# Transposes issued by SyncE instead of ScalarE, value planes prepared one weight tile sooner, and a shorter last normalisation, in a one-core streaming encoder layer

## The chip, the core and the metric

The kernel runs on one core of a Trainium2 chip. The core has five engines, each with its own instruction queue that runs in order: TensorE (PE in the profile, its weight loads as PEld), VectorE (DVE), ScalarE (ACT), GpSimd (POOL) and SyncE (SP), which only issues transfers. Sixteen DMA engines move data between HBM and the on-chip memory SBUF, for all queues together. SyncE, ScalarE and GpSimd can issue DMAs. The metric is device time in microseconds for one execution.

## The reference

One layer of a streaming encoder is applied to two request groups that share the weights: 256 new frames of a prompt and 64 next frames of a running stream with 256 cached rows of keys and values. Inputs and weights are float32, and the model width is 2048.

```python
def layer(x, l, cache_k, cache_v, ...):
    xn = rmsnorm(x, norm_mix[l])
    proj = xn @ w_in[l]
    q, k, v, u, vs, g = jnp.split(proj, ...)      # 8 heads x 128 each for q, k, v; 1024 for u, vs; 4096 for g
    a = stick_breaking(...)                       # prompt: own keys; sample: cache + own keys
    u = jax.nn.gelu(u)
    vs = rmsnorm(jax.nn.gelu(vs), sgu_norm[l])
    bb = spatial_gate(u, vs, w_spatial[l], b_spatial[l])
    gates = jax.nn.sigmoid(g + b_gate[l])
    merged = g_a * (a @ w_branch_a[l]) + g_b * (bb @ w_branch_b[l])
    h = x + merged @ w_out[l]
    gu = rmsnorm(h, norm_ffn[l]) @ w_gate_up[l]
    h = h + (silu(gu[..., :D_FF]) * gu[..., D_FF:]) @ w_down[l]     # D_FF = 5632
    return h, k, v, vs

def stick_breaking_block(q_blk, q_pos, k, v, k_pos):
    z = einsum(q_blk, k) * (SB_HEAD_DIM ** -0.5)
    mask = k_pos[None, :] < q_pos[:, None]
    log_beta = log_sigmoid(z)
    log_stay = where(mask, log_sigmoid(-z), 0.0)
    log_rest = cumsum(log_stay, reverse=True) - log_stay
    w = where(mask, exp(log_beta + log_rest), 0.0)
    return einsum(w, v)
```

The outputs are the final RMSNorm of `h` for both groups, the new k and v rows of both, and the normalised `vs` rows of the sample.

## The kernel before

**Layout.** Features lie on the 128 partitions, and the T = 320 frames (256 prompt, 64 sample) lie along the free dimension. A weight matrix is cut into blocks of 128 output columns; for every such block the kernel walks the contraction in *weight tiles* of eight 128x128 blocks (512 KB). `weights` (line 74) loads a tile on SyncE into a buffer `raw`, and `halved` (line 66) splits it in two: `wh`, a rounded copy that ACT writes (line 69, a "cast"), and `wl`, the rest, which VectorE computes (line 70, a "split"). Activations are split the same way. `product` (line 83) then issues three matmuls for each 128x128 block: high by high, high by low, low by high (lines 86 to 88), so that float32 accuracy is kept on a faster number format. A tile therefore feeds 24 matmuls of 320 columns.

**Buffers.** There are three `raw` buffers, and three more (`raw2`) while the attention pool is open, and four each of `wh` and `wl`. A new weight tile is issued when the split of an older tile has freed its buffer. A cast waits until TensorE has done with an older `wh`.

**Ticks.** `block` (line 90) computes one block of 128 output columns, and after each weight tile it calls `tick()`. Other work is hung on later ticks with `at(tick, function, ...)`: it is then traced between two weight tiles. Which instruction of an engine goes first is decided when the program is built, by when each is expected to be ready; `keep_in_program_order` pins an instruction behind what was traced before it on its engine. At run time each queue is fixed and runs in order.

**Attention.** Heads are treated in pairs p = 0 to 3. After a pair's k, q and v blocks, `attend` (line 380) hangs up its steps: `att_scores` (TensorE, masks, and the activations on ACT), `att_sums` (the reversed running sums, on VectorE), `att_values`, `att_weights`, `att_plane`, `att_join` and `att_out`. The attention weights `w` and the values `v` must be transposed. Both are float32, and the DMA transpose moves 16-bit elements, so each is taken as two 16-bit *planes*:

- `turn_begin` (line 260), called by `att_values` for the values, and by `sgu_turn` for the rows of the spatial gate: four ACT copies collect the planes of two heads in `flat` (lines 264 and 267), then one DMA transpose writes `turned` (line 269, issued by ACT). `turn_end` puts the planes together again on VectorE (line 277).
- `att_weights` applies the exponential on ACT (line 318) and calls `att_plane(p, 0)`; two ticks later comes `att_plane(p, 1)`. Each copies one plane of `w` into `e` on ACT (line 326) and transposes it into `c` (line 327, issued by ACT).
- `att_join` (line 329) puts the planes of `c` together on VectorE (line 334) and calls `turn_end` for the values. `att_out` (line 340) is the product with the values.

There are 16 transposes: two of `c` and one of `turned` for each of four pairs, and four of `turned` for the spatial gate, about 70 to 317 us after the start.

**The end.** The last `w_down` slice adds to `hs[m]` block by block (line 536). The squares of blocks 0 to 14 are summed in `sqf.total`, those of the last block stand in `last` (line 544), and each `hs[m]` is multiplied by its gain (line 545). Then six matmuls against a column of ones sum both square tiles over the partitions, into one PSUM bank (line 551). ACT takes the square root of the mean (line 553), VectorE writes the mean itself (line 554), and `newton` (line 130: a reciprocal and three small steps, lines 131 to 134) makes an accurate reciprocal root `r`, one value per frame, with frames on partitions. To bring `r` back along the free dimension, VectorE scales an identity by it (`diag`, line 559) and TensorE multiplies a matrix of ones by that (line 560). Sixteen VectorE multiplies of 128x320 (line 562) and nine DMAs issued by SyncE (line 566) follow. A float32 matmul appears as two passes in the profile.

Of the kernel before, what the change touches and what calls it, by code (L numbers as in the profile page):

```python
# [8 lines left out]
F32 = mybir.dt.float32  # L9
F32R = mybir.dt.float32r  # L10
U16 = mybir.dt.uint16
AF = mybir.ActivationFunctionType
ALU = mybir.AluOpType

P = 128
TP = 256
TS = 64
T = TP + TS
D = 2048
KD = D // P  # L20
# [6 lines left out]
EPS = 1e-6  # L27
# [6 lines left out]
def stream_step(ctx: ExitStack, tc: tile.TileContext, xT, w_in, w_a, w_b, w_out, w_gu, w_down,  # L34
                gains, ws_t, bs, ck_t, cv, y_t, k_t, v_t, sv_t):
    nc = tc.nc
# [5 lines left out]
    tmp = pool("tmp", 2)  # L42
# [5 lines left out]
    def aux():  # L48
        return psum.tile([P, 512], F32, tag="aux", bufs=4, name="aux")

    def aux1():
        return psum.tile([P, 512], F32, tag="aux1", bufs=1, name="aux1")
# [4 lines left out]
    def at(tick, fn, *a):  # L57
        assert tick > state["tick"], (tick, state["tick"])
        later.setdefault(tick, []).append((fn, a))
# [30 lines left out]
    def block(src, act):  # L90
        ps = acc()
        nk = len(act)
        for k0 in range(0, nk, HALF):
            n = min(HALF, nk - k0)
            w = weights(src[:, k0 * P : (k0 + n) * P], n)
            for j in range(n):
                product(ps, w, j, act[k0 + j], k0 + j == 0, k0 + j == nk - 1)
            tick()
        return ps[:, :T]
# [4 lines left out]
    def pair(name, shape=(2, T), dt=F32):  # L104
        return big.tile([P, *shape], dt, tag="D", bufs=24, name=name)
# [8 lines left out]
    def t320(tag, bufs=2, dt=F32):  # L114
        return tmp.tile([P, T], dt, tag=tag, bufs=bufs, name=tag)

    ones = const.tile([P, P], F32, name="ones")
# [5 lines left out]
    eps_t = const.tile([P, 1], F32, name="eps_t")  # L123
# [3 lines left out]
    ident = const.tile([P, P], F32, name="ident")  # L127
    make_identity(nc, ident)

    def newton(r, ms, e):  # L130
        nc.vector.reciprocal(out=r, in_=r)
        nc.vector.scalar_tensor_tensor(out=e, in0=ms, scalar=-0.5, in1=r, op0=ALU.mult, op1=ALU.mult)
        nc.vector.tensor_tensor(out=e, in0=e, in1=r, op=ALU.mult)
        nc.vector.scalar_tensor_tensor(out=r, in0=e, scalar=1.5, in1=r, op0=ALU.add, op1=ALU.mult)
# [125 lines left out]
    def turn_begin(t2):  # L260
        hw = t2.bitcast(U16).rearrange("p j (t w) -> p j t w", w=2)
        flat = pair("flat", (2, 5 * P), U16)
        for i in range(2):
            c = nc.scalar.copy(out=flat[:, i, 0:512].rearrange("p (j t) -> p j t", j=2), in_=hw[:, :, 0:TP, 1 - i])
            if i == 0:
                tc.keep_in_program_order(c)
            nc.scalar.copy(out=flat[:, i, 512:640].rearrange("p (j t) -> p j t", j=2), in_=hw[:, :, TP:T, 1 - i])
        turned = pair("turned", (2, 5, P), U16)
        nc.scalar.dma_start_transpose(out=turned.rearrange("p i b d -> p (i b) d"),
                                      in_=flat.rearrange("p i t -> p (i t)"))  # L270
        return turned

# [43 lines left out]
    def att_weights(p):  # L316
        w = attn[p]["w"]
        tc.keep_in_program_order(nc.scalar.activation(out=w, in_=w, func=AF.Exp))
        att_plane(p, 0)

    def att_plane(p, i):
        s = attn[p]
        hw = s["w"].bitcast(U16).rearrange("p (n w) -> p n w", w=2)
        flat = s["e"].bitcast(U16).rearrange("p (i n) -> p i n", i=2)
        to = s["c"].bitcast(U16).rearrange("p (i n) -> p i n", i=2)
        tc.keep_in_program_order(nc.scalar.copy(out=flat[:, i, :], in_=hw[:, :, 1 - i]))
        nc.scalar.dma_start_transpose(out=to[:, i, :].rearrange("p (b q) -> p b q", q=P), in_=flat[:, i, :])

    def att_join(p):
        s = attn[p]  # L330
# [6 lines left out]
    def att_values(p):  # L337
        attn[p]["turned"] = turn_begin(attn[p]["v"])
# [41 lines left out]
    def attend(p, now):  # L380
        at(now + 1, att_scores, p)
        at(now + 3, att_sums, p)
        at(now + 5, att_values, p)
        at(now + 8, att_weights, p)
        at(now + 10, att_plane, p, 1)
        at(now + 11, att_join, p)
        at(now + 12, att_out, p)

    for name, b in (("q", 0), ("k", 1), ("v", 2)):
        for h in range(2):  # L390
            head_out(name, first[h][b][:, :T], h)
    at(state["tick"] + 4, mix_load)
    attend(0, state["tick"] + 1)
    for h in range(2, H):
        if h % 2 == 0:
            attn[h // 2] = {}
            at(state["tick"] + 4, att_load, h // 2)
        for name, b in (("k", 1), ("q", 0), ("v", 2)):
            head_out(name, block(w_in[b * H + h], xs), h)
        if h % 2:  # L400
            attend(h // 2, state["tick"])
# [9 lines left out]
    for g in range(H):  # L411
        ps = block(w_in[4 * H + g], xs)
        t = t320("ev")
# [11 lines left out]
    def sgu_turn(p):  # L425
        for j in range(2):
            g, v = 2 * p + j, vs[p][:, j, :]
            nc.vector.scalar_tensor_tensor(out=v, in0=v, scalar=g_sgu[:, g : g + 1], in1=got["rv"],
                                           op0=ALU.mult, op1=ALU.mult)
            nc.gpsimd.dma_start(out=sv_t[g], in_=v[:, TP:T])  # L430
        turns[p] = turn_begin(vs[p])
# [33 lines left out]
    for g in range(H):  # L465
        ps = block(w_in[3 * H + g], xs)
        t = t320("ev")
# [5 lines left out]
    for m in range(KD):  # L473
        gate = []
        for i in range(2):
            ps = block(w_in[5 * H + i * KD + m], xs)
            t = t320("ev")
# [8 lines left out]
        ps = block(w_a[m], aT)  # L486
        t = t320("mg", 1)
        nc.vector.tensor_tensor(out=t, in0=ps, in1=gate[0], op=ALU.mult)
        ps = block(w_b[m], bT)
# [8 lines left out]
    hs, ypair, hg = [], [], []  # L498
    sq = Squares("sq_h")
    for m in range(KD):  # L500
# [4 lines left out]
        ps = block(w_out[m], merged)  # L505
# [7 lines left out]
    sqf = Squares("sq_f")  # L513
    last = const.tile([P, T], F32, name="last")
    for s0, n in SLICES:
# [18 lines left out]
        for m in range(KD):  # L534
            ps = block(w_down[m][:, s0 * P : (s0 + n) * P], act)
# [9 lines left out]
            nc.vector.tensor_scalar(out=hs[m], in0=hs[m], scalar1=g_fin[:, m : m + 1], scalar2=None, op0=ALU.mult)  # L545

    spans = ((192, slice(2, 3)), (0, slice(0, 1)), (128, slice(1, 2)))
    ps = aux1()
    for t0, c in spans:
        for i, t in enumerate((sqf.total, last)):  # L550
            nc.tensor.matmul(ps[:, c], t[:, t0 : t0 + P], ones[:, 0:1], start=i == 0, stop=i == 1)
    ms, r, e = (const.tile([P, 3], F32, name=f"col{i}") for i in range(3))
    nc.scalar.activation(out=r, in_=ps[:, 0:3], func=AF.Sqrt, bias=eps_t, scale=1.0 / D)
    nc.vector.tensor_scalar(out=ms, in0=ps[:, 0:3], scalar1=1.0 / D, scalar2=EPS, op0=ALU.mult, op1=ALU.add)
    newton(r, ms, e)
    rf = aux()
    for t0, c in spans:
        d = tmp.tile([P, P], F32, tag="diag", bufs=3, name="diag")
        nc.vector.tensor_scalar(out=d, in0=ident, scalar1=r[:, c], scalar2=None, op0=ALU.mult)
        nc.tensor.matmul(rf[:, t0 : t0 + P], ones, d, start=True, stop=True)  # L560
    for i in range(KD):
        nc.vector.tensor_tensor(out=hs[i], in0=hs[i], in1=rf[:, :T], op=ALU.mult)  # L562
    done = 0
    for n in (1, 1, 2, 2, 2, 2, 2, 2, 2):
        y = ypair[done // 2][:, done % 2 : done % 2 + n, :]
        nc.sync.dma_start(out=y_t[:, done : done + n, :], in_=y)
        done += n

# [54 lines left out]
```

## Time and profile before

| | |
|---|---|
| timed runs | 1712.06, 1713.77, 1714.26 us (median 1713.77) |
| the profiled execution | 1716.95 us |
| its span, first to last instruction | 1715.2 us |
| mean granted TensorE clock | 0.995 |
| VectorE waiting for transposes of c (line 334) | 15.0 us, 7 times, longest 4.5 |
| VectorE waiting for transposes of turned (line 277) | 13.1 us, 5 times, longest 8.4 |
| transposes of c, issue to landing, median (8) | 7.3 us |
| transposes of turned, issue to landing, median (8) | 4.8 us |
| a weight tile of w_in, issue to landing, median | 3.6 us |

The profile is of one execution. A row of the timeline has the start, the duration, the engine and line, the operation, what it writes and reads, how many instructions are merged into the row, and in brackets the idle time of the engine before it and what ended that. An engine's name with q (SPq, ACTq) is its instruction queue: issuing a DMA or waiting, not computing. In the chain of waits a row has the start, the time that the step takes in the chain, and the step. In the view by windows a row has the stretch, its length, the busy time and count of instructions of each engine (PE, PEld, DVE, ACT, POOL), TensorE's granted clock, the mean busy share of the 16 DMA engines and the GB/s that they moved. In the list of waits a row has who waited for whom, the total, the number of times, and the longest.

### The profile page before, as it was taken

To read this page: it belongs to the slowest core of one execution; us is meant where nothing else is said; L and a number is where in the kernel's file an instruction comes from. 1 tells how busy PE (TensorE), PEld (TensorE's weight loads), DVE (VectorE), ACT (ScalarE), POOL (GpSimd) and SP (SyncE) were. 2 spreads that over 40 slices of the span, in tenths; PEclk is the share of its full clock that TensorE was granted. 3 is DMA by queue.
4 is the path that set the end of the run, shared out by engine and by line. 5 is a ranking of instruction groups with operands and counts; after the bars stand their busy time and mean duration, and the time that the engine had idled before them with its cause. 6 is when DMAs were issued, how large, how long until landed. Compare 5 with 4: busy or idle time off the path is not lost.

```text
span 1715.2 us, 27292 instructions
## 1 busy us (share of the span) xinstructions
PE 1696.7 (99%) x11538; PEld 1691.5 (99%) x11538; DVE 867.9 (51%) x1077; ACT 664.1 (39%) x811; POOL 56.4 (3%) x89
## 2 busy tenths in 40 slices
PE   9999999999999999999999999999999999999996
PEld 9999999999999999999999999999999999999996
DVE  7655547544444445555444444444444444444454
ACT  6544455433333334444333332333333323333442
POOL 0200011000000001220000000000000000000000
PEclk9999999999999999999999999999999999999998
DMA  8767655444444445554444444444444444444443
GB/s 290 236 160 170 163 164 167 116 152 152 150 148 148 152 150 165 172 166 148 149 154 151 150 148 149 150 153 151 149 148 150 150 154 150 148 148 150 138 149 105
DMA packets 97355, 268.30 MB, mean 156 GB/s; under 512 B 28976, under 2 KB 31280, under 8 KB 97232
## 3 DMA queue, kind: packets, MB, share of 16 engines
q1 hardware_dynamic: 74496, 253.26, 46.0%
q10 hardware_dynamic: 20112, 5.03, 2.3%
q0 software_dynamic: 2624, 8.26, 1.5%
q8 instruction: 90, 1.47, 0.3%
q14 instruction: 33, 0.27, 0.0%
HBM read 256.03 MB, written 5.51 MB: 152 GB/s over the span
## 4 chain that ended last, share of the span: by engine, by line
PE 97%; DMA 1%; DVE 1%; ACT 0%; issue 0%; SPq 0%; ACTq 0%; DVEq 0%
PE acc L86 31%; PE acc L88 31%; PE acc L87 31%; DMA c<-e 1%; PE aux L88 1%; PE aux L86 1%; PE aux L87 1%; DVE h L562 0%; DMA x<-xT 0%; PE aux L350 0%; PE aux L442 0%; PE aux L286 0%; PE aux L347 0%; PE aux L289 0%; PE aux L285 0%
## 5 line engine op out<-in xcount | busy, mean ns | idle before, releaser
L69 ACT CAST wh<-raw 128x1024 fp32r<-128x1024 f32 (+1 forms) x484 | 497.5, 1029 | 978.2 <-PE acc L87 773.9
L70 DVE TENSOR_TENSOR wl<-raw,wh 128x1024 fp32r<-128x1024 f32 (+1 forms) x484 | 579.2, 1198 | 482.6 <-ACT wh L69 482.2
L88 PE MATMUL acc<-A,wl 128*128 128x320 f32 x2496 | 772.2, 309 | 3.0 <-DVE wl L70 3.0
L86 PE MATMUL acc<-A,wh 128*128 128x320 f32 x2496 | 774.1, 310 | 1.0 <-ACT A L109 1.0
L87 PE MATMUL acc<-A,wh 128*128 128x320 f32 x2496 | 772.0, 309 | 0.2 <-DVE A L110 0.2
L88 PEld LDWEIGHTS acc<-A,wl 128*128 128x128 f32 x2496 | 469.0, 188 | 3.8 <-DVE wl L70 3.7
L86 PEld LDWEIGHTS acc<-A,wh 128*128 128x128 f32 x2496 | 469.2, 188 | 3.0 <-issue 1.5
L87 PEld LDWEIGHTS acc<-A,wh 128*128 128x128 f32 x2496 | 469.3, 188 | 0.6 <-DVE A L110 0.4
L88 PE MATMUL acc<-act,wl 128*128 128x320 f32 x704 | 217.5, 309 | 0.0
L86 PE MATMUL acc<-act,wh 128*128 128x320 f32 x704 | 217.5, 309 | 0.0
L87 PE MATMUL acc<-act,wh 128*128 128x320 f32 x704 | 217.5, 309 | 0.0
L86 PEld LDWEIGHTS acc<-act,wh 128*128 128x128 f32 x704 | 132.1, 188 | 0.0
L87 PEld LDWEIGHTS acc<-act,wh 128*128 128x128 f32 x704 | 132.1, 188 | 0.0
L88 PEld LDWEIGHTS acc<-act,wl 128*128 128x128 f32 x704 | 132.1, 188 | 0.0
L86 PE MATMUL acc<-mh,wh 128*128 128x320 f32 x256 | 79.1, 309 | 0.0
L87 PE MATMUL acc<-ml,wh 128*128 128x320 f32 x256 | 79.1, 309 | 0.0
L88 PE MATMUL acc<-mh,wl 128*128 128x320 f32 x256 | 79.1, 309 | 0.0
L523 DVE TENSOR_TENSOR bb<-acc,rh 128x320 f32<-128x320 f32 x44 | 21.6, 492 | 57.5 <-PE acc L88 57.5
L520 DVE TENSOR_TENSOR ev<-acc,rh 128x320 f32<-128x320 f32 x44 | 21.6, 492 | 56.6 <-PE acc L88 56.6
L536 DVE TENSOR_TENSOR h<-acc,h 128x320 f32<-128x320 f32 x48 | 23.5, 489 | 49.6 <-PE acc L88 49.6
L86 PEld LDWEIGHTS acc<-mh,wh 128*128 128x128 f32 x256 | 48.0, 188 | 0.0
L87 PEld LDWEIGHTS acc<-ml,wh 128*128 128x128 f32 x256 | 48.0, 188 | 0.0
(176 smaller groups left out, 1084.5 us busy)
## 6 DMA issues: line engine op xcount, KB each, us to landing
raw<-w_gu SPq DMA_DIRECT2D x176, 512.0 KB, 3.5
raw<-w_in SPq DMA_DIRECT2D x141, 512.0 KB, 3.6
raw<-w_down SPq DMA_DIRECT2D x80, 512.0 KB, 3.5
raw<-w_out SPq DMA_DIRECT2D x32, 512.0 KB, 3.6
raw<-w_a SPq DMA_DIRECT2D x16, 512.0 KB, 3.5
raw<-w_b SPq DMA_DIRECT2D x16, 512.0 KB, 3.5
raw<-w_down SPq DMA_DIRECT2D x16, 256.0 KB, 2.7
xr<-xT POOLq DMA_DIRECT2D x16, 160.0 KB, 2.6
```

What stands on the lines that cost most here:

```text
L69: nc.scalar.copy(out=wh[:, : n * P], in_=raw[:, : n * P])
L70: nc.vector.tensor_tensor(out=wl[:, : n * P], in0=raw[:, : n * P], in1=wh[:, : n * P].bitcast(F32), op=ALU.subtract)
L86: nc.tensor.matmul(ps[:, :T], a, x[0], start=first, stop=False)
L87: nc.tensor.matmul(ps[:, :T], a, x[1], start=False, stop=False)
L88: nc.tensor.matmul(ps[:, :T], b, x[0], start=False, stop=last)
L520: nc.vector.tensor_tensor(out=t, in0=pg, in1=got["rh"], op=ALU.mult)
L523: nc.vector.tensor_tensor(out=u, in0=pu, in1=got["rh"], op=ALU.mult)
L536: nc.vector.tensor_tensor(out=hs[m], in0=ps, in1=hs[m], op=ALU.add)
```

## The change

1. Both transposing DMAs (lines 269 and 327) are issued by SyncE instead of ScalarE, in the same queue as the weight tiles.
2. `att_values` is hung on the fourth tick after a pair's last block instead of the fifth.
3. At the end, the sums of `sqf.total` and of `last` go to a PSUM bank each (three matmuls each, the first three traced before the others). VectorE scales the first sum and adds the second to it, and ACT takes the root of that result.
4. The identity is no longer scaled. TensorE takes `r` itself, broadcast along the free dimension with step zero, as the weights, and multiplies the identity by it.
5. The final multiplies run just before each output DMA, over one or two blocks at a time: nine instead of sixteen.

```diff
@@ turn_begin
         turned = pair("turned", (2, 5, P), U16)
-        nc.scalar.dma_start_transpose(out=turned.rearrange("p i b d -> p (i b) d"),
+        nc.sync.dma_start_transpose(out=turned.rearrange("p i b d -> p (i b) d"),
                                       in_=flat.rearrange("p i t -> p (i t)"))
@@ att_plane
         tc.keep_in_program_order(nc.scalar.copy(out=flat[:, i, :], in_=hw[:, :, 1 - i]))
-        nc.scalar.dma_start_transpose(out=to[:, i, :].rearrange("p (b q) -> p b q", q=P), in_=flat[:, i, :])
+        nc.sync.dma_start_transpose(out=to[:, i, :].rearrange("p (b q) -> p b q", q=P), in_=flat[:, i, :])
@@ attend
-        at(now + 5, att_values, p)
+        at(now + 4, att_values, p)
@@ the end
-    ps = aux1()
-    for t0, c in spans:
-        for i, t in enumerate((sqf.total, last)):
-            nc.tensor.matmul(ps[:, c], t[:, t0 : t0 + P], ones[:, 0:1], start=i == 0, stop=i == 1)
+    sums = aux(), aux()
+    for ps, t in zip(sums, (sqf.total, last)):
+        for t0, c in spans:
+            nc.tensor.matmul(ps[:, c], t[:, t0 : t0 + P], ones[:, 0:1], start=True, stop=True)
     ms, r, e = (const.tile([P, 3], F32, name=f"col{i}") for i in range(3))
-    nc.scalar.activation(out=r, in_=ps[:, 0:3], func=AF.Sqrt, bias=eps_t, scale=1.0 / D)
-    nc.vector.tensor_scalar(out=ms, in0=ps[:, 0:3], scalar1=1.0 / D, scalar2=EPS, op0=ALU.mult, op1=ALU.add)
+    nc.vector.tensor_scalar(out=ms, in0=sums[0][:, 0:3], scalar1=1.0 / D, scalar2=EPS, op0=ALU.mult, op1=ALU.add)
+    nc.vector.scalar_tensor_tensor(out=ms, in0=sums[1][:, 0:3], scalar=1.0 / D, in1=ms, op0=ALU.mult, op1=ALU.add)
+    nc.scalar.activation(out=r, in_=ms, func=AF.Sqrt)
     newton(r, ms, e)
     rf = aux()
     for t0, c in spans:
-        d = tmp.tile([P, P], F32, tag="diag", bufs=3, name="diag")
-        nc.vector.tensor_scalar(out=d, in0=ident, scalar1=r[:, c], scalar2=None, op0=ALU.mult)
-        nc.tensor.matmul(rf[:, t0 : t0 + P], ones, d, start=True, stop=True)
-    for i in range(KD):
-        nc.vector.tensor_tensor(out=hs[i], in0=hs[i], in1=rf[:, :T], op=ALU.mult)
+        nc.tensor.matmul(rf[:, t0 : t0 + P], r[:, c].to_broadcast([P, P]), ident, start=True, stop=True)
     done = 0
     for n in (1, 1, 2, 2, 2, 2, 2, 2, 2):
         y = ypair[done // 2][:, done % 2 : done % 2 + n, :]
+        nc.vector.tensor_tensor(out=y, in0=y, in1=rf[:, None, :T].to_broadcast([P, n, T]), op=ALU.mult)
         nc.sync.dma_start(out=y_t[:, done : done + n, :], in_=y)
         done += n
```

## The prediction

> **What bounds the kernel now.** I read the page first: span, busy times and DMA queues.
>
> ```profile
> span 1715.2 us, 27292 instructions
> PE 1696.7 (99%) x11538; PEld 1691.5 (99%) x11538; DVE 867.9 (51%) x1077; ACT 664.1 (39%) x811; POOL 56.4 (3%) x89
> ...
> q10 hardware_dynamic: 20112, 5.03, 2.3%
> ```
>
> TensorE is the bound. The matmuls are not touched by the change, except a few in the last 15 us, so only two things can be gained: holes in the matmul stream, and the end, where the stream is over. q10 is ACT's DMA queue: 5 MB, which are the transposes; the weights go by SP's.
>
> For the holes I read the timeline of PE and the list of waits. One hole is large, and it lies in the attention of head pair 2 (p = 2):
>
> ```profile
> 180.77 0.31 PE L86 MATMUL acc<-A,wh 128*128 128x320 f32 x1
> ...
> 181.80 0.31 PE L87 MATMUL acc<-A,wh 128*128 128x320 f32 x1
> 185.11 0.42 PE L88 MATMUL acc<-A,wl 128*128 128x320 f32 x1 [3.00 <-DVE wl L70]
> ```
>
> The start times 180.77 to 181.80 span seven steps, so a matmul is issued every 0.147 us; eight k-blocks of three matmuls make 3.53 us for a weight tile. Between 181.80 and 185.11 lie 3.31 us, 3.16 more than a step. The chain of waits through the same place tells why, and what follows:
>
> ```profile
> 165.69 16.96 DMA c<-e
> ...
> 183.85 1.22 DVE wl L70
> ...
> 186.43 0.27 PE acc L86
> 186.30:189.60 3.30, 3.30 (x14) 3.30 (x13) 3.30 (x4) 0.30 (x1) 0.54 (x1) 0.50 0.82 280
> ```
>
> (The last row is of the view by windows: the granted clock, third from the end, is 0.50 there.) From 186.3 a matmul takes 0.27 us instead of 0.147, for 3.3 us: 3.3 x (1 - 0.147 / 0.27) = 1.5 us lost. The hole thus costs 3.2 + 1.5 = **4.7 us**, and its root is a transpose of 17 us, for which VectorE, ACT and SP stood still in turn:
>
> ```profile
> 162.83 1.63 ACTq L269 DMA_TRANSPOSE turned<-flat  x1
> 165.69 2.95 ACTq L327 DMA_TRANSPOSE c<-e  x1
> 170.87 5.62 ACTq L327 DMA_TRANSPOSE c<-e  x1
> 176.60 2.94 ACT L69 CAST wh<-raw 128x1024 fp32r<-128x1024 f32 x3 [5.76 <-issue]
> 176.63 0.54 DVE L277 COPY rows<-turned 128x640 uint16<-128x640 uint16 x1 [8.37 <-DMA turned<-flat]
> 182.74 0.81 DVE L334 COPY w<-c 128x1152 uint16<-128x1152 uint16 x1 [4.47 <-DMA c<-e]
> 167.89 10.74 SPq L80 DMA_DIRECT2D raw<-w_in  x2
> ```
>
> ACT spent 5.62 us on issuing one transpose (a cast behind it idled 5.76 us). VectorE waited 8.37 and 4.47 us for landings, with the next splits (wl, line 70) queued behind. The last row says that SP issued only two weight tiles in 10.7 us, since no split had freed a buffer.
>
> Why 17 us? Two rows of the view by windows (the last three columns are PE's clock, the DMA share and GB/s), then c's time from issue to landing, over the kernel and for pair 3 alone:
>
> ```profile
> 164.00:176.00 12.00, 12.00 (x84) 12.00 (x83) 1.63 (x2) 4.20 (x4) 0.57 (x1) 1.00 1.20 105
> 400.00:412.00 12.00, 12.00 (x84) 12.00 (x83) 6.57 (x8) 4.43 (x6) 0.00 (x0) 1.00 0.46 156
> DMA to landing us min/median/max: 3.2/7.3/17.0
> DMA to landing us min/median/max: 3.2/4.3/5.3
> ```
>
> From 164 to 176 the 16 DMA engines are full by their records (1.20) and move 105 GB/s; with weights alone (400 to 412) a share of 0.46 moves 156. In pair 3 a transpose of c lands in 3.2 and 5.3 us. So transposes and weight tiles, in flight together from two queues, slow each other.
>
> **The change, part by part.**
>
> *Transposes on SP's queue.* No transpose is added: 8 of c and 8 of turned leave ACT's queue and enter SP's. A transpose then follows the weight tiles issued ahead of it and precedes those behind. If the queue runs in order, the mixture of 164 to 176 is gone, apart from POOL's writes: a transpose waits for the tile ahead and then runs as in pair 3. For pair 2, with the slower 5.3 us from pair 3 each time: turned, 164 to 169, instead of 176.6; c, 165.7 to 171 (now 182.65) and 170.9 to 176.2. VectorE's copies (0.81, 0.54) and the split (1.22) put PE's tile at about 179, while PE needs it at 181.95 (one step after 181.80): 3 us of cover. The hole goes: **-4.7 us**. What is last then is PE itself, on these numbers.
>
> What it costs SP: each issue takes 1.3 to 5.6 us as it did on ACT, and queued behind it are weight tiles only, one per 3.53 us. The cover is the tiles already loaded:
>
> ```profile
> ACT wh L69 <- PE acc L87: 773.9, 357, 2.8
> ACT wh L69 <- DMA raw<-w_in: 1.3, 3, 0.7
> ```
>
> In the whole kernel the casts waited 1.3 us for weights, and mostly for PE; even in SP's 10.7 us with two issues, three casts ran back to back at 176.60. A hold on SP of up to about 10 us is therefore free. If that cover went, a late tile would cost PE what it is late, plus half-speed matmuls as above. ACT gains 16 issues that it does not need.
>
> The Trainium skill speaks against this: "DMA: Bandwidth & Descriptors", section "Issuing engines are not separate DMA queues", says that DMAs of any issuing engine run on the same 16 engines and interleave, so that another issuer saves only issue time. The rows of 164 to 176 agree that they share and interleave. By that rule alone the hole would stay, and the sum would be the end's gain only (rival 1, priced from rows).
>
> *Values' planes one tile sooner.* Four ACT copies per pair and the issue of turned move past one cast, 3.5 us ahead.
>
> ```profile
> 162.50 0.30 ACT L267 COPY flat<-v 128x128 uint16<-128x128 uint16 x1
> 162.70 1.17 ACT L318 ACTIVATE w<-w 128x1152 f32<-128x1152 f32 x1
> ```
>
> The last of the four starts 0.20 us ahead of what follows, and the 512-column ones, four times as wide, need no more than four times that: at most 2 us, by which the cast comes later; casts wait 773.9 us for PE in all: 0. It adds margin to the term above; alone it cannot close a 17 us transpose. I take 0, bounds -0.5 to +0.5 (a quarter of the 2 us, should the shift show once).
>
> *The end.* The chain from the last squares on:
>
> ```profile
> 1699.86 1.29 PE aux L551 x10
> ...
> 1701.47 0.16 DVE col L554
> ...
> 1701.75 0.17 DVE col L132
> ...
> 1702.34 0.30 DVE diag L559
> 1702.68 1.66 PE aux L560 x6
> 1704.37 6.45 DVE L562 TENSOR_TENSOR h<-h,aux 128x320 f32<-128x320 f32 x16 [1.35 <-PE aux L560]
> 1709.00:1712.00 3.00, 0.00 (x0) 0.00 (x0) 1.82 (x5) 0.00 (x0) 0.00 (x0) 0.50 1.01 389
> ```
>
> - Sums in two banks: four of the ten passes after 1699.86 belong to the other squares and run earlier, while ACT squares the last tile. 10 passes in 1.29 us, about 0.11 each: -0.44.
> - The mean now goes through VectorE ahead of ACT: an operation of 0.17 (as line 132's) and a hand-over of 0.02. Behind ACT, lines 554 and 131 take 0.28 now (1701.47 to 1701.75); the reciprocal alone, at line 132's step of 0.20, saves 0.08: +0.11.
> - No diag ahead of the first broadcast: -0.34.
> - Six passes with r as step-zero weights: the trace has no such weight load. Nearest row: 1.66 us for six passes at half clock. If the clock is still full they take, as an estimate from the two speeds above, some 0.6 less; if such a load took double, 1.4 more. I take 0.
> - 16 multiplies of 0.40 (6.45 in all) become 2 of 0.40 and 7 of about 0.73 (a 128x640 multiply, `mix`, is below; less 0.09 of overlap): 5.9 instead of 6.4. But in the last row the DMA engines are full (1.01) at 389 GB/s: the writes set the end, and 0.5 less on VectorE brings only the sooner start of the first pair, 0.06.
>
> ```profile
> L452 DVE TENSOR_TENSOR mix<-mix,us 128x640 f32<-128x640 f32 x4 | 3.3, 818 | 0.0
> ```
>
> Sum of the end: -0.44 + 0.11 - 0.34 - 0.06 = **-0.7**, bounds -1.6 (full clock, half of VectorE's gain) and +0.7 (double loads).
>
> **Sum.** -4.7 - 0.7 = -5.4. The profiled execution took 1716.95 us (span 1715.2 and 1.75 around it): 1711.55 after. Against the median of the timed runs, 1713.77, it is **1708.4**. The profiled one lies 3.2 above that median; if all of this were a larger hole under the profiler, timed runs would hold only 1.5 of the 4.7. I take the full 4.7, the only hole that a row measures, and keep 1.5 as the other end.
>
> **Rivals.**
>
> 1. *The mixture stays.* Transposes share the engines with weights from one queue as from two, or the order between SP's tiles is such that the landing times stay. For it: share 1.20 above. Against: pair 3's 3.2 us, and one queue cannot overtake itself. Only the end counts: 1713.8 - 0.7 = 1713.1. The change then does not do what it says.
> 2. *The hole is smaller in timed runs.* Then -1.5 - 0.7: 1711.6. For it: the 3.2 us between profile and median. Against: the span's other parts may differ as well.
> 3. *Slower: SP held by a transpose whose plane is not ready.* ACT's copies sit behind casts that wait for PE; weight tiles would queue behind the transpose at SP. Three issues of 1.63, 2.95 and 5.62 make 10.2 us, just under the 10.7 that the buffers bore; any wait for a plane on top runs the casts dry. It decides once SP is held over 10.7 us. Then the old hole stays and one tile is late by 3.5, with 1.5 of half clock: +5.0 - 0.7 = +4.3, 1718.1. A hold that the buffers bear costs nothing, so below that point this rival is worth 0.
>
> **How the numbers follow.** About 0.2%, 3.4 us, is what a measurement of this kernel can tell from no change: faster is below 1710.3, slower above 1717.2. Forecast, 1708.4: chance 0.53; its own range is 1706.0 (end at -1.6, planes at -0.5, and 1.0 for the spread of runs: before, the fastest lies 1.7 under the median) to 1710.3. Rival 1: 0.20. Rival 2: 0.17, a little of it under 1710.3. Rival 3: 0.10. Faster 0.55, same 0.35, slower 0.10. The range takes in rivals 1 and 2: 1706.0 to 1713.4.
>
> **What would show each step.** In the changed profile q10 should be nearly empty and the transposes stand as issues of SP. Right: c and turned of pair 2 land in 3 to 7 us, no 3 us gap in PE near 182, no clock of 0.50 before the end, VectorE's waits for c and turned mostly gone. Wrong: landings above 10 us, casts that wait for weights, a new half-clock stretch. At the end: six passes of line 551's successor after the last square instead of ten, no diag, the broadcast passes 0.7 sooner after the last square, and the last write landing only as much sooner as the first. The forecast falls if transposes behind weight tiles are slow in one queue too, or if the timed runs never had the hole.

## The result, and the profile after

| | before | after |
|---|---|---|
| timed runs, median | 1713.18 us | 1710.47 us |
| lowest and highest, 22 runs each | 1711.0 to 1716.92 | 1709.53 to 1712.23 |
| the profiled execution | 1716.95 | 1710.77 |
| its span | 1715.2 | 1708.9 |

The ratio of the times is 0.9984, with a 95% interval of 0.9977 to 0.9990. The change makes the kernel faster by 2.7 us, or 0.16%: the interval leaves out "no change", and the gain stays under the 0.2% that the prediction called the least that can be told. It forecast 5.4 us. The runs of before spread over 5.9 us, those of the changed kernel over 2.7.

The page of the changed kernel, the same lines as before: span, busy times, DMA queues. q10 is almost empty, since the transposes went to SyncE's queue q1.

```profile
span 1708.9 us, 27292 instructions
PE 1695.0 (99%) x11538; PEld 1690.1 (99%) x11538; DVE 867.1 (51%) x1068; ACT 664.4 (39%) x811; POOL 55.9 (3%) x89
...
q1 hardware_dynamic: 94464, 258.25, 47.7%
...
q10 hardware_dynamic: 144, 0.05, 0.0%
```

The view by windows, the stretch that held the hole (columns as before), and then the list of waits:

```profile
164.00:176.00 12.00, 12.00 (x84) 12.00 (x83) 6.00 (x8) 5.23 (x5) 0.57 (x1) 1.00 0.86 192
100.00:250.00 150.00, 150.00 (x1024) 147.82 (x1023) 83.62 (x114) 79.39 (x98) 12.84 (x18) 1.00 0.60 167
DVE w L334 <- DMA c<-e: 12.1, 4, 4.9
DVE rows L277 <- DMA turned<-flat: 7.8, 4, 2.2
ACT wh L69 <- DMA raw<-w_in: 1.5, 3, 1.0
```

From 164 to 176 the DMA engines move 192 GB/s instead of 105. TensorE is busy for all 150 us of the attention, and the clock stays at 1.00. VectorE still waits up to 4.9 us for c (4.5 before), and for turned 2.2 (8.4 before), but TensorE waits only 0.3 us in the whole kernel for a split (3.0 before). The casts wait 1.5 us for weights, against 1.3: SyncE's transposes did not run them dry.

Pair 2 in the timeline of SyncE, then the times from issue to landing of turned and of c in that stretch:

```profile
156.99 2.04 SPq L269 DMA_TRANSPOSE turned<-flat  x1
162.21 1.86 SPq L80 DMA_DIRECT2D raw<-w_in  x2
164.12 2.05 SPq L327 DMA_TRANSPOSE c<-e  x1
166.31 0.49 SPq L80 DMA_DIRECT2D raw<-w_in  x1
169.62 1.30 SPq L327 DMA_TRANSPOSE c<-e  x1
DMA to landing us min/median/max: 5.2/5.2/5.2
DMA to landing us min/median/max: 3.7/5.3/7.0
```

The transposes stand between weight tiles and land in 3.7 to 7.0 us, where they took 12.4 to 17.0. Turned is issued at 157.0 (162.8 before), so it has landed at 162.2, before c is issued at 164.1. That is two changes at once, one queue and no overlap of turned with c; the experiments separate them.

The end, in the chain of waits:

```profile
1693.70 0.16 PE acc L88
...
1694.94 0.84 PE aux L551 x6
...
1696.44 0.17 DVE col L132
...
1697.05 1.66 PE aux L559 x6
...
1698.74 0.49 DVE h L563
```

Six passes stand between the last squares and the mean, not ten. No scaled identity stands before the broadcast, whose six passes with step-zero weights take 1.66 us, exactly what the old six took.

### The profile page after: what moved, and what is told of

It is laid out like the page before. It is cut to its first block, busy times and chain, and to the rows that moved or that the text cites. A ratio compares the mean times of both kernels' runs of the same rounds, so it can differ in the third digit from the quotient of the medians.

```text
span 1708.9 us, 27292 instructions
## 1 busy us (share of the span) xinstructions
PE 1695.0 (99%) x11538; PEld 1690.1 (99%) x11538; DVE 867.1 (51%) x1068; ACT 664.4 (39%) x811; POOL 55.9 (3%) x89
## 4 chain that ended last, share of the span: by engine, by line
PE 99%; DVE 1%; DMA 0%; issue 0%; ACT 0%; SPq 0%; DVEq 0%
PE acc L86 32%; PE acc L88 32%; PE acc L87 32%; PE aux L86 0%; PE aux L88 0%; PE aux L87 0%; DVE h L563 0%; DMA x<-xT 0%; PE aux L350 0%; PE aux L442 0%; PE aux L286 0%; PE aux L347 0%; PE aux L289 0%; DVE wl L70 0%; PE aux L285 0%
```

## The experiments

The prediction's theory, A: weights and transposes in flight from two queues slow each other, and one queue cures it. Its rivals were B, that the sooner planes are the cure, and that timed runs hold a smaller hole than the profiled one. Each kernel was timed beside runs of the kernel before on the same chip. Pair 2's landings are those of turned and of the two transposes of c.

| run | median (range), runs | before, beside it (range) | ratio, 95% interval | pair 2's landings, us | gap in TensorE near 180 us |
|---|---|---|---|---|---|
| before, profile shown | 1713.18 (1711.0-1716.9), 22 | | | 13.8, 17.0, 12.4 | 3.00 |
| transposes only | 1711.18 (1710.3-1713.2), 11 | 1712.63 (1711.0-1717.3) | 0.9985-1.0002 | 7.8, 7.3, 5.6 | none |
| values only | 1712.23 (1711.8-1713.3), 11 | the same runs | 0.9989-1.0007 | 5.6, 6.3, 4.1 | none |
| end only | 1712.15 (1711.1-1716.0), 11 | the same runs | 0.9988-1.0006 | 13.2, 14.6, 10.7 | 1.34 |
| all but the end | 1711.70 (1710.8-1712.8), 11 | the same runs | 0.9985-1.0002 | 6.0, 8.0, 4.8 | none |
| changed, again | 1710.17 (1709.4-1711.6), 12 | 1713.20 (1710.9-1718.6) | 0.9966-0.9986 | 5.5, 8.2, 5.0 | none |
| changed, clock kept | 1710.87 (1709.5-1711.7), 12 | the same runs | 0.9973-0.9994 | 6.0, 7.7, 4.4 | none |
| changed, without the transposes' move | 1710.72 (1710.0-1712.9), 12 | 1713.01 (1710.9-1718.7) | 0.9978-0.9996 | 5.9, 6.6, 4.5 | none |

### Each part alone

**Transposes alone.**

```diff
-        nc.scalar.dma_start_transpose(...)      # turned, line 269; c, line 327
+        nc.sync.dma_start_transpose(...)
```

> Only the two transposing DMAs move from ScalarE's queue to SyncE's. Theory A (weights and transposes in flight from two queues slow each other; one queue keeps them apart): the transposes of pair 2 land in 3 to 7 us instead of 13.8, 17.0 and 12.4, no gap over 1 us in the matmul stream between 100 and 250 us, no half clock there, and the run is 1 to 2 us faster than before (the whole change gives 2.7, its end 1.3 by the traces). Rival B (the earlier planes of the values are what closes the hole): landings stay above 10 us and the gap stays at about 3 us.

The hole is gone in the profiled execution, as theory A has it. The median is 1.45 us under that of before, inside the expected 1 to 2, but with 11 runs the interval still includes no change. In this kernel turned and c overlap as they did before (issued at 165.9, 168.0 and 171.8), in one queue. By windows:

```profile
166.00:178.00 12.00, 12.00 (x83) 12.00 (x83) 6.02 (x8) 6.05 (x6) 0.57 (x1) 1.00 1.12 214
DMA to landing us min/median/max: 7.8/7.8/7.8
DMA to landing us min/median/max: 5.6/6.4/7.3
```

The DMA share is as full as in the slow stretch of before (1.12 against 1.20), but it moves 214 GB/s, not 105. The last two rows are turned's and c's times to landing.

This execution took 1713.21 us, the longest of its eleven, though it has no hole. At its start its matmuls ran at half clock for 3.4 us:

```profile
9.20:12.60 3.40, 3.40 (x15) 3.40 (x15) 3.35 (x7) 3.10 (x7) 0.00 (x0) 0.50 1.04 378
```

So the hole is not the only thing that makes one execution longer than another.

**Values alone.**

```diff
-        at(now + 5, att_values, p)
+        at(now + 4, att_values, p)
```

> Only the values' planes are prepared one weight tile sooner; transposes stay on ScalarE's queue. Theory A: the landing times of pair 2 stay near those of before (above 8 us in at least one transpose), a hole of 0 to 5 us remains, time within 1.5 us of before. Rival B: transposes land in 3 to 7 us, no hole, 1 to 2 us faster.

Here theory A failed. The transposes are still ScalarE's, yet pair 2 has no hole:

```profile
L269 ACTq DMA_TRANSPOSE turned<-flat x1: 1752/1752/1752, 157.1 to 157.1; - x1
DMA to landing us min/median/max: 5.6/5.6/5.6
L327 ACTq DMA_TRANSPOSE c<-e x2: 1671/1795/1919, 163.8 to 169.7; - x2
DMA to landing us min/median/max: 4.1/5.2/6.3
164.00:176.00 12.00, 12.00 (x84) 12.00 (x84) 6.95 (x10) 5.26 (x5) 0.81 (x2) 1.00 0.95 215
```

Turned is issued 6.7 us before c and lands first (157.1 + 5.6 = 162.7, c at 163.8). ScalarE's issue of each takes 1.7 to 1.9 us, not up to 5.6. Rival B's landings came out; its gain of 1 to 2 us did not (0.4 in the medians, within the noise). Each cure alone closes the hole in the one execution seen of it.

**The end alone.**

```diff
 # the new end of the change; lines 269, 327 and 383 as before
-        nc.sync.dma_start_transpose(...)
-        at(now + 4, att_values, p)
+        nc.scalar.dma_start_transpose(...)
+        at(now + 5, att_values, p)
```

> Only the end is changed. By the traces of before and after, the stretch from the start of the last matmul of the weights (line 88) to the end of the span shrinks from 16.7 to 15.4 us: 1.3 us faster in time, with the hole of pair 2 as in before. The prediction's own sum would give 0.7. Rival: the 1.3 was the luck of one execution, then 0.7 or less.

The medians differ by 0.5 us, which the interval does not tell from 0 or from 1.3. Its trace tells more: from the end of the last weight matmul to the last landing it takes 14.12 us against 15.05 in the profile of before. Of these 0.93 us, 0.17 are a broadcast that ran partly at full clock, so the new end is worth 0.76, and not the 1.3 expected; the rest of the 1.3 is another speed of the last writes (see the last section). The run also tells of the hole: the front is the kernel before, with slow landings again (10.7 to 14.6), but TensorE idles only 1.34 us and its clock does not fall. Its runs spread as those of before do, up to 1716.0.

**All but the end.**

> The whole change but for its end: transposes on SyncE's queue and the planes one tile sooner. If the parts simply add, it is 1.3 us slower than the changed kernel, so 1.0 to 1.8 us faster than before, without a hole. Theory A: as fast as with the transposes alone, within 0.5 us, since the sooner planes only add cover. Rival B: clearly faster than with the transposes alone, by 1 us or more.

It is 0.9 us under the median of before and 0.5 above the transposes alone: the second cure adds nothing that these runs can tell, as expected. (Its edit is the first two diffs together.)

### Repeats

> The changed kernel once more, beside the kernel before on the same chip: 1 to 3 us faster; its runs spread over less than 3.5 us, those of before over 5 us or more, if the hole is what makes runs of before differ. Landings of pair 2 under 8 us and no hole in a second execution.

Confirmed: 3.0 us faster, ratio 0.9976, runs within 2.2 us where those of before spread over 7.7. No hole in a second execution; one landing, 8.2, is just over the 8 expected.

> The kernel before, a second profile. If the hole differs from execution to execution (it was 4.7 us in the profile shown and 1.6 in the run with the end alone), it is another size here, between 0 and 5 us, and the run's time follows it about one to one; if it is fixed, it is 4.5 to 5 us again.

The hole does differ between executions. The prediction shows the first matmul after it, at 185.11, with 3.00 us of TensorE's idle time in brackets. The same row in TensorE's timeline of this execution, and then of the end alone:

```profile
184.53 0.42 PE L88 MATMUL acc<-A,wl 128*128 128x320 f32 x1 [1.69 <-DVE wl L70]
```

```profile
184.41 0.41 PE L88 MATMUL acc<-A,wl 128*128 128x320 f32 x1 [1.34 <-DVE wl L70]
```

With 3.00 the clock fell for 3.3 us; with 1.69 and 1.34 it did not. These executions took 1716.95, 1714.42 and 1713.78 us. The first two differ by 2.5 us, against 1.3 of idle time and 1.5 of half clock, so the time follows the hole about one to one. The first is at the top of the 22 runs of before.

### Which queue, which issuer

Since either cure suffices, the theory became D: what is slow is two transposes in flight at once while weight tiles come by another queue. Its rival E: what is slow is ScalarE as the issuer. Four kernels changed the queues, all with the old place of the values and the old end.

```diff
-        nc.sync.dma_start(out=raw[:, : n * P], in_=src)
+        (nc.OTHER if LOW <= state["tick"] < 42 else nc.sync).dma_start(out=raw[:, : n * P], in_=src)
```

| transposes by | weights around pairs 1 and 2 by | pair 1's landings, us | pair 2's landings, us |
|---|---|---|---|
| ScalarE | SyncE (before) | 8.7, 11.3, 7.7 | 13.8, 17.0, 12.4 |
| SyncE | SyncE (transposes only) | 6.9, 6.2, 5.1 | 7.8, 7.3, 5.6 |
| SyncE | ScalarE, pair 2 alone (LOW 30) | (one queue) | 6.3, 5.1, 3.7 |
| SyncE | GpSimd (LOW 16) | 9.4, 11.9, 9.5 | 5.3, 7.7, 6.3 |
| ScalarE | GpSimd (LOW 16) | 8.9, 6.7, 4.6 | 7.5, 6.9, 5.8 |
| ScalarE | ScalarE (LOW 16) | 3.4, 3.2, 3.6 | 3.4, 4.0, 3.7 |

> The transposes go by SyncE's queue with the values' planes at their old place, as in the run with the transposes alone, but the twelve weight tiles loaded around pair 2 go by ScalarE's queue: the two queues of before with their loads swapped. Theory D (what is slow is two transposes in flight at once while weight tiles come by another queue; either cure alone suffices): pair 2's transposes land in over 9 us again, against 5.6 to 7.8 us with the transposes alone. Rival E (only ScalarE's issue of the transposes matters, through the casts behind it): they stay at 5 to 8 us. ScalarE may be held by weight tiles that wait for a buffer, so the run's time itself decides nothing.

The landings stayed low, against theory D. But ScalarE's queue, held by its other work, issued no weight tile between 162.3 and 167.2, just when turned and c overlapped. One tile was in flight beside them, where before had two, so the run lacked part of the load that it was to bring; the next ones put the weights on GpSimd's queue.

> The kernel before with the transposes on SyncE's queue and 26 weight tiles (those loaded around pairs 1 and 2) on GpSimd's queue; the values' planes at their old place, so that the transposes of turned and of c overlap. Again two queues, now with a weight tile started within a microsecond of turned, which the run with weights on ScalarE's queue lacked. Theory D (two queues at once, with two transposes queued on one of them): pair 2's transposes land in over 9 us. Rival E (it takes ScalarE as the issuer): 5 to 8 us.

> As the kernel before, transposes on ScalarE's queue, but the same 26 weight tiles on GpSimd's queue. Theory D: over 9 us, as in the run before it in this list. Rival E: over 9 us here and 5 to 8 us there. If both stay under 8 us, what is slow needs SyncE's and ScalarE's queues together, the two whose transfers hardware queues issue.

> As the kernel before, but the same 26 weight tiles go by ScalarE's queue, where the transposes are: one queue, and ScalarE the issuer. Theory D: 4 to 8 us. Rival E: over 9 us. ScalarE may be held by tiles that wait for a buffer, so the time of the run decides nothing.

Rows of pair 1: first SyncE's transposes beside GpSimd's weights, then everything by ScalarE.

```profile
L269 SPq DMA_TRANSPOSE turned<-flat x1: 1894/1894/1894, 115.6 to 115.6; - x1
DMA to landing us min/median/max: 9.4/9.4/9.4
L327 SPq DMA_TRANSPOSE c<-e x2: 2127/2401/2675, 118.7 to 122.2; - x2
DMA to landing us min/median/max: 9.5/10.7/11.9
```

```profile
L269 ACTq DMA_TRANSPOSE turned<-flat x1: 1337/1337/1337, 115.3 to 115.3; - x1
DMA to landing us min/median/max: 3.4/3.4/3.4
L327 ACTq DMA_TRANSPOSE c<-e x2: 1318/1568/1818, 117.9 to 122.0; - x2
DMA to landing us min/median/max: 3.2/3.4/3.6
```

Rival E falls: SyncE's transposes were as slow in pair 1 as ScalarE's had been. The 3.2 to 4.0 us with everything by ScalarE decide nothing: its queue issued no weight tile between 108.1 and 119.8, nor between 155.1 and 167.7, so none was in flight while turned and the first c overlapped. One queue under load is seen with SyncE alone (5.1 to 7.8 us in two pairs). Theory D is half borne out: every landing of a transpose over 8.2 us, in all profiles, is of two queues and overlapping transposes. But pair 2 stayed under 8 us with GpSimd's weights, so these two conditions don't suffice. By the second run's expectation it would then take the queues of SyncE and ScalarE together, but in pair 1 SyncE's and GpSimd's gave 9.4 to 11.9. What third condition makes 17 us of 8 stays open. None of the three had a hole near 180 us.

The profiled executions of the last three took 1710.70, 1711.96 and 1710.75 us, beside one run of before at 1717.05; the run with weights on ScalarE around pair 2 had a median of 1712.01, in 8 runs. None tells more than that no hole stood in it.

### The clock at the end, and the change without its name-giving part

```diff
     for ps, t in zip(sums, (sqf.total, last)):
         for t0, c in spans:
             nc.tensor.matmul(ps[:, c], ...)
+        for _ in range(fill):        # 2, then 6
+            nc.tensor.matmul(idle[:, :T], filler[:, :P], filler, start=True, stop=True)
```

> The changed kernel with eight more matmuls of 128x320 that compute nothing that is used, in the two idle stretches of TensorE at the end: two after the first three sums, six after the others. If the half clock of the broadcast passes comes from the idle time before them, the clock stays 1.00 through them and the first multiply comes some 0.6 us sooner after the last matmul of the weights (4.5 instead of 5.0 to 5.2); time 0 to 1 us below the changed kernel. Rival: the clock falls all the same or the fillers delay the sums, then 0 to 0.5 us slower.

The broadcast passes took 0.95 us. So they did in the second execution of the changed kernel, without fillers. The rows are of the chain, first of the changed kernel again, then of the kernel with fillers:

```profile
1693.93 0.16 PE acc L88
...
1697.28 0.95 PE aux L559 x6
1698.25 0.49 DVE h L563
```

```profile
1694.52 0.16 PE acc L88
...
1697.87 0.95 PE aux L562 x6
1698.84 0.49 DVE h L566
```

From the end of the last weight matmul to the first multiply, both need 4.16 us. The fillers' worth is inconclusive from these, and the time, 1710.87, is no better than 1710.17.

Last, the changed kernel with `nc.scalar` in lines 269 and 327 again:

> The changed kernel with its transposes back on ScalarE's queue: the sooner planes and the new end alone. If the sooner planes suffice to close the hole, as in the run with them alone, no gap over 1 us stands between 100 and 250 us, pair 2's transposes land in 4 to 8 us, and its time is within 0.7 us of the changed kernel's (some 2 to 3 us faster than before, spread of the runs below 3.5 us). If the move of the transposes brings something of its own, it is 1 us or more slower than the changed kernel, with a spread like that of before.

No hole, landings 4.5 to 6.6 us, and 2.3 us faster than before (ratio 0.9987), 0.25 above the changed kernel's first median and 0.55 above its second, in other runs. So once the planes come sooner, the move to SyncE's queue brings nothing that these medians can tell. One thing differs in the traces: here the last write lands 3.39 us after its issue, in the changed kernel 2.81 and 2.82 (see the last section). No version beat the changed kernel clearly.

## Why the prediction was right, and where it was not

The measured 1710.47 lies in the range of 1706.0 to 1713.4, and the sign was right. But it lies there because the range took in rivals 1 and 2: the forecast's own range ended at 1710.3. The forecast of 1708.4 was too low, and half of its gain came. It gave 0.55 to a gain of over 0.2%, and the gain was 0.16%.

- **Bound.** Right: TensorE is busy 99% before and after, and what was gained is a hole and the end.
- **The hole, -4.7 us.** This term was mis-sized. In the profiled pair it came out in full: the last weight matmul ended 4.93 us sooner (1693.86 against 1698.79). But the step "I take the full 4.7, the only hole that a row measures" failed: other executions of the same front had 1.34 and 1.69 us of idle time and no half clock. Of the 2.7 us in the medians the traces give 0.76 to the new end and 0.57 to a faster last write (both below), which leaves 1.4 for the hole. That is a subtraction, not a measurement. The runs with the old end and one cure or both gained 0.4 to 1.45 us (the two with transposes on SyncE with the faster last write in it), each with an interval that takes in no change; the changed kernel with its transposes on ScalarE gained 2.3, less 0.76 for the end 1.5. Rival 2, the smaller hole in timed runs, fits best: it said 1.5 for the hole and, counted from the three runs of before at 1713.77, 1711.6 for the time. No timed run was traced, so their holes were not seen. The sign stood in the numbers: the profiled execution lay 3.2 us over the median of the timed ones.
- **Why the transposes are fast in one queue.** Right as a cure, too narrow as a cause. Of the sooner planes it said "alone it cannot close a 17 us transpose", which was wrong: alone they brought 17.0 down to 6.3. The slow landings stood only where turned and c were in flight together beside weights of another queue, and either undoing their overlap or putting all in one queue removed them. Pair 3 of the kernel before, which the prediction took as its measure, could have told: its transposes too ran beside weight tiles of SyncE's queue. Such a tile, in flight from 216.0 to 220.5, is the row below; c, issued at 219.3 with no other transpose in flight, landed in 3.2 us. So weights and transposes from two queues are not slow as such.

```profile
L80 SPq DMA_DIRECT2D raw<-w_in x1: 328/328/328, 216.0 to 216.0; - x1
DMA to landing us min/median/max: 4.5/4.5/4.5
```

- **The arithmetic of pair 2** (landings of 5.3 us, 3 us of cover): the transposes alone, the fair test of it, had 5.6 to 7.8. The hole closed, though with longer landings than the term assumed.
- **Rival 1 and the page behind it.** The Trainium skill, "DMA: Bandwidth & Descriptors", section "Issuing engines are not separate DMA queues", has all DMAs share and interleave on the same 16 engines, whoever issues them. The runs agree that the issuer as such does not matter (pair 1 beside weights of another queue: 7.7 to 11.3 us by ScalarE, 9.4 to 11.9 by SyncE). They disagree that another issuer saves only issue time: moving the transposes to the weights' queue raised 105 GB/s to 214 in a stretch as full.
- **Rival 3.** It did not come. SyncE issued transposes in 1.3 to 2.1 us around pair 2, and casts waited 1.5 us for weights in the whole kernel.
- **The end, -0.7 us.** Right, piece by piece. Ten passes of 1.29 us became six of 0.84: -0.45 (predicted -0.44). From the sums to line 132 it takes 0.66 us (1695.78 to 1696.44) against 0.60: +0.06 (+0.11). The diag's 0.34 is gone. The step-zero weights cost nothing. Up to the first multiply that makes 4.88 us after the last weight matmul instead of 5.58: -0.70. From there on the prediction gave 0.06, because the writes set the end. The profiled pair has more, 8.84 us to the last landing against 9.47. The prediction's sign, a last write that lands only as much sooner as the first, did not come: the first landed 5.62 us sooner, the last 6.27. The new end is not the cause. With the same speed of the last writes (next but one section) the old end needs 8.90 us in the transposes alone against 8.84, and 9.47 in before against 9.42 in the end alone: 0.05 to 0.06, as predicted. The other 0.57 goes with the writes' speed, a term that the sum did not have.

## What to carry to other kernels

A stall read from one profile is one draw: before pricing it, compare the profiled time with the median and the spread of the timed runs, and where the profiled one lies near the slowest, price the stall at what the median can hold. When a change removes two conditions of a stall at once, run each alone before crediting either; here one moved tick closed the hole as well as the move of sixteen transposes did. And see that DMA transposes do not overlap each other while bulk loads come by another queue. Last, when time at the end changes, see which queues worked there before crediting the new code: here 0.57 us went with a packet that no line of the end issues.

## What the runs showed of the hardware

**Full DMA engines at half the rate.** With turned and c in flight on one queue and weight tiles on another, the records of the 16 engines were full (1.20) at 105 GB/s; the same transfers in one queue were as full (1.12) at 214. Two queues and overlapping transposes stood in every case of a transpose that took over 8.2 us, but not each such case was slow.

**The half clock at the end falls at different points.** The broadcast's six passes took 1.66 us in the profile of the changed kernel, 0.95 in its second, and 1.49 in the kernel with the end alone (granted clock 0.71 in the mean there). That is up to 0.7 us of a run's end.

```profile
1699.00:1701.30 2.30, 1.48 (x6) 1.18 (x6) 0.63 (x5) 0.00 (x0) 0.00 (x0) 0.71 0.00 0
```

The Trainium skill's page "TensorE: Matmul & The Clock Gate", section "What's actually happening", says that the clock is set by a window of 3413 ns that runs freely and does not start anew with the kernel. The runs agree that the same program meets the drop at different points, and the two half-clock stretches shown, after the hole of before (3.3 us) and at the start of the transposes alone (3.4 us), are about as long as one such window.

**The last writes have two speeds, which go with the program.** With the old end the ninth write, the last, landed 3.0 us after its issue in four profiles (both of before among them) and 2.4 in five. With the new end it took 3.4 in two profiles and 2.8 in three (both of the changed kernel among them). No program showed both speeds. Where all weights come by SyncE's queue, the slower speed stood in all five profiles with transposes by ScalarE, the faster in all five with transposes by SyncE. The rows are the landing times of the nine writes and the DMA queues that worked during them, first of before, then of the transposes alone.

```profile
DMA to landing us min/median/max: 1.8/2.3/3.0
q1 hardware_dynamic: 1296, 2.62, 66.9%
q14 instruction: 1, 0.01, 0.2%
```

```profile
DMA to landing us min/median/max: 1.8/2.3/2.4
q1 hardware_dynamic: 1296, 2.62, 71.2%
```

In all six slow profiles one packet of the instruction queue q14 starts during the writes, at 1710.5 us in before, and the first write to land after it, 0.6 us later, is the first late one. In the eight fast ones no such packet starts before the last landing. So moving the transposes seems to have moved a load of instructions out of the way of the output; no run moved that packet alone, and why it falls where it does stays open. The 0.57 us between the two speeds is nearly as much as the whole new arithmetic of the end brings.
